# A column-sum kernel on one core: the first load takes nine rows instead of one and then eight, and the split of the last rows moves from 352 to 384 columns

## The chip, the cores and the metric

The kernel runs on one core of a Trainium2 chip. The metric is the device time in microseconds; the time before is 628.3 us (three runs, 628.29 to 628.32). A second number comes with every run: the span, from the first to the last instruction that the profiler records. It is printed to 0.1 us, and before's time is some 1.8 us longer than its span (628.3 against 626.5).

## The reference

```python
grad_output = np.random.randn(32, 1024, 2048).astype(np.float32)

def reference(grad_output):
    return np.sum(grad_output, axis=(0, 1)).astype(np.float32)
```

32,768 rows of 2048 fp32, 268.4 MB, are summed into one row. A row is 8 KB.

## The kernel before

SyncE issues all loads. A load of m rows per partition gives every partition m rows that follow each other in memory, so it is 128 pieces of m x 8 KB. A ring of three slots of eight rows takes 30 tiles; VectorE adds each tile into itself and carries two rows over to the next tile. One odd row (the "head") lies at the start of slot 2, where the first tile looks for the rows carried over. Fifteen rows per partition follow the tiles: VectorE adds seven of them, TensorE the other eight and VectorE's sum (products with a column of ones). The last three are loaded in a left part and a right part, so that little is left to do after the last byte.

```python
LEFT = ((0, 424, 0), (424, 424, 1), (848, 424, 2), (1272, 424, 3))
RIGHT = ((1696, 176, 2), (1872, 176, 3))
...
    ring = const_pool.tile([P, SLOTS * TILE * D], fp32)
...
    def load(m, dst, lane, after=None, first=None, lo=0, hi=D):
        ...
        src = flat[first : first + P * m].rearrange("(p m) d -> p m d", p=P)[:, :, lo:hi]
        loads.append((dst.rearrange("p (m d) -> p m d", m=m), src, lane, after))

    head_at = 2 * TILE
    load(1, rows(head_at, 1), head_in)
    for k in range(TILES):
        s = k % SLOTS
        load(TILE, rows(s * TILE, TILE), slot_in[s], (vec, k - 1) if k >= 2 else None)
...
    nc.vector.memset(psum[:], 0.0).then_inc(zero, 1)
    nc.vector.memset(rows(head_at + 1, WIDE - 1), 0.0)
    nc.vector.wait_ge(head_in, 16)
    with nc.vector.Fori(0, LOOPS):
        for s in range(SLOTS):
            at, before = s * TILE, (s - 1) % SLOTS * TILE
            take(nc.vector, slot_in[s])
            settle()
            vadd(at, rows(before, WIDE), WIDE).then_inc(vec, 1)
            ...
```

## Time and profile before

| what | before |
|---|---|
| time, span | 628.3 us, 626.5 us |
| first DMA issued, first packet | 0.89 us, 1.92 us |
| tile 0 in, on the first and on the last of 16 DMA engines | 24.65 us, 25.16 us |
| last load in, on the first and on the last engine | 622.46 us, 622.93 us |

Rows 2 to 4 come from the trace's packet records (start, duration, size) and from its records of semaphore increments: a load's semaphore rises once for each of the 16 DMA engines, so the trace tells when each engine's share of a load was in. The next lines are the timeline of before after the last load; columns are start, duration, engine and line, operation, and in brackets the idle time in front with what ended it.

```profile
622.97 0.09 PEld L199 LDWEIGHTS psum<-ring,ones 128*1 128x1 f32 x4 [0.22 <-DMA ring<-in_grad_output_dram]
623.21 0.64 SPq L232 DMA_DIRECT2D out_dram<-ring  x1
623.47 0.33 DVE L230 COPY ring<-psum 1x176 f32<-1x176 f32 x1 [3.28 <-PE psum L199]
623.51 0.30 ACT L230 COPY ring<-psum 1x176 f32<-1x176 f32 x1 [0.33 <-PE psum L199]
623.90 0.37 SPq L233 DMA_DIRECT2D out_dram<-ring  x1
```

The weight load of TensorE (PEld) at 622.97 us waited for a DMA: it starts 0.04 us after the last engine's share of the last load.

### The profile page before, as it was taken

The page shows a single profiled execution, that of the slowest core. Times are in us where ns is not written, and L with a number is a line of the kernel's source. Part 1 is how long each engine was busy: PE and PEld are TensorE (multiplying, and loading weights), DVE is VectorE, ACT ScalarE, POOL GpSimd, SP SyncE. Part 2 cuts the span into 40 slices and gives each one's busy share as a digit, 9 for nine tenths or more (in the row PEclk, how much of TensorE's full clock was granted, in tenths as well). Part 3 has the DMA queues.
Part 4 walks back from the last instruction along what each step waited for, and adds up shares of the span by engine and source line. Part 5 has one row for each costly group of instructions (what it writes and reads, how often), then busy time and mean ns, then how long its engine had stood idle before and what let it go on. Part 6 is the DMA issues. An engine that isn't in the chain of part 4 may idle for free. (4 is left out here: it accounts for less than half of the span.)

```text
span 626.5 us, 563 instructions
## 1 busy us (share of the span) xinstructions
PE 11.3 (2%) x108; PEld 3.4 (1%) x108; DVE 547.7 (87%) x102; ACT 2.3 (0%) x4; POOL 0.3 (0%) x5
## 2 busy tenths in 40 slices
PE   0000000000000000000000000000000000000007
PEld 0000000000000000000000000000000000000002
DVE  1389888899888898888988889888899888899996
ACT  0000000000000000000000000000000000000000
POOL 0000000000000000000000000000000000000000
PEclk9999999999999999999999999999999999999999
DMA  9999999999999999999999999999999999999997
GB/s 402 402 469 402 469 402 469 402 469 402 464 406 460 410 423 448 418 452 414 456 402 469 402 469 402 469 402 469 402 469 402 464 406 439 431 423 448 427 410 303
DMA packets 5755, 268.46 MB, mean 429 GB/s; under 512 B 629, under 2 KB 1018, under 8 KB 1402
## 3 DMA queue, kind: packets, MB, share of 16 engines
q1 hardware_dynamic: 5754, 268.45, 99.2%
q8 instruction: 1, 0.02, 0.0%
HBM read 268.44 MB, written 0.01 MB: 429 GB/s over the span
## 5 line engine op out<-in xcount | busy, mean ns | idle before, releaser
L122 DVE TENSOR_TENSOR ring<-ring 128x4096 f32<-128x4096 f32 (+2 forms) x93 | 528.9, 5687 | 71.0 <-DVEq L116 63.7
L199 PE MATMUL psum<-ring,ones 128*1 128x424 f32 (+1 forms) x108 | 11.3, 513 | 612.1 <-DMA ring<-in_grad_output_dram 612.0
L180 DVE TENSOR_TENSOR ring<-ring 128x6784 f32<-128x6784 f32 (+5 forms) x6 | 15.8, 2646 | 0.2
L199 PEld LDWEIGHTS psum<-ring,ones 128*1 128x1 f32 x108 | 3.4, 89 | 619.7 <-DMA ring<-in_grad_output_dram 614.2
L230 DVE COPY ring<-psum 1x176 f32<-1x176 f32 x1 | 0.3, 334 | 3.3 <-PE psum L199 3.3
L225 ACT COPY ring<-psum 128x424 f32<-128x424 f32 x1 | 0.5, 512 | 620.3 <-PE psum L199 620.3
L142 DVE MEMSET ring<- 128x2048 f32 x1 | 1.8, 1765 | 0.4 <-issue 0.4
L141 DVE MEMSET psum<- 128x1024 f32 x1 | 0.9, 912 | 1.2 <-POOLq L125 1.2
L222 ACT ACT_TABLE_LOAD x1 | 1.3, 1283 | 0.9 <-PEq L252 0.9
L230 ACT COPY ring<-psum 1x176 f32<-1x176 f32 x1 | 0.3, 300 | 0.3 <-PE psum L199 0.3
L222 ACT COPY warm<-ones 1x1 f32<-1x1 f32 x1 | 0.2, 190 | 0.0
L252 POOL MEMSET const-bfloat16-1.0<- 128x1 bf16 x1 | 0.1, 101 | 0.0
L252 POOL MEMSET const-uint8-127<- 128x1 uint8 x1 | 0.1, 101 | 0.0
L129 POOL MEMSET ones<- 128x1 f32 x1 | 0.1, 99 | 0.5 <-POOLq L125 0.5
L252 POOL MEMSET const-float32-0.0<- 128x1 f32 x1 | 0.1, 98 | 0.2 <-issue 0.2
L252 POOL MEMSET const-float32-1.0<- 128x1 f32 x1 | 0.1, 98 | 0.0
## 6 DMA issues: line engine op xcount, KB each, us to landing
ring<-in_grad_output_dram SPq DMA_DIRECT2D x1, 7168.0 KB, 33.3
ring<-in_grad_output_dram SPq DMA_DIRECT2D x1, 3072.0 KB, 21.8
ring<-in_grad_output_dram SPq DMA_DIRECT2D x1, 2048.0 KB, 26.4
ring<-in_grad_output_dram SPq DMA_DIRECT2D x1, 1696.0 KB, 30.0
ring<-in_grad_output_dram SPq DMA_DIRECT2D x1, 1024.0 KB, 4.9
ring<-in_grad_output_dram SPq DMA_DIRECT2D x1, 848.0 KB, 31.3
ring<-in_grad_output_dram SPq DMA_DIRECT2D x3, 176.0 KB, 31.1
ring<-in_grad_output_dram SPq DMA_DIRECT2D x30, 34.1
```

The costliest lines, as they stand in the source:

```text
L122: return nc.vector.tensor_add(out=rows(at if to is None else to, n), in0=rows(at, n), in1=other)
L129: nc.gpsimd.memset(ones[:], 1.0).then_inc(one, 1)
L141: nc.vector.memset(psum[:], 0.0).then_inc(zero, 1)
L142: nc.vector.memset(rows(head_at + 1, WIDE - 1), 0.0)
L180: add = nc.vector.tensor_add(out=x, in0=x, in1=grid[:, m:n, lo:hi])
L199: mat = nc.tensor.matmul(sums[lo], lhsT=ones[:], rhs=ring[:, x : x + n], start=start, stop=then is not None)
L222: nc.scalar.copy(out=warm[:], in_=ones[0:1, :])._wait_ge(one, 1)
L225: nc.scalar.copy(out=res, in_=psum[:, :n])._wait_ge(mm_left, len(LEFT)).then_inc(left, 1)
L230: copy(out=dst, in_=sums[lo])._wait_ge(mm_right, i + 1).then_inc(right, 1)
L252: nc = _bacc.Bacc("TRN2", target_bir_lowering=False, num_devices=1)
```

## The change

The first load takes nine rows at once into a store with one row of room ahead of the ring, on tile 0's semaphore; VectorE copies the odd row to where the first tile looks for it. That saves a DMA and a semaphore. And the right part of the last three rows is 384 columns wide, which puts the starts and ends of both parts on multiples of 512 B (1664 x 4 B = 13 x 512 B).

```diff
-LEFT = ((0, 424, 0), (424, 424, 1), (848, 424, 2), (1272, 424, 3))
-RIGHT = ((1696, 176, 2), (1872, 176, 3))
+LEFT = ((0, 416, 0), (416, 416, 1), (832, 416, 2), (1248, 416, 3))
+RIGHT = ((1664, 192, 2), (1856, 192, 3))
...
-    ring = const_pool.tile([P, SLOTS * TILE * D], fp32)
+    store = const_pool.tile([P, (1 + SLOTS * TILE) * D], fp32)
+    head, ring = store[:, :D], store[:, D:]
...
-    head_in, more_in = tc.alloc_semaphore("head"), tc.alloc_semaphore("more")
+    more_in = tc.alloc_semaphore("more")
...
     head_at = 2 * TILE
-    load(1, rows(head_at, 1), head_in)
-    for k in range(TILES):
+    load(1 + TILE, store[:, : (1 + TILE) * D], slot_in[0])
+    for k in range(1, TILES):
...
-    nc.vector.wait_ge(head_in, 16)
+    nc.vector.wait_ge(slot_in[0], 16)
+    nc.vector.tensor_copy(out=rows(head_at, 1), in_=head)
```

Nine rows are 73,728 B per partition, and the built kernel moves them as two pieces of 36,864 B.

## The prediction

> **What bounds the kernel now.** I read four views, in this order: the page's strip of 40 slices with the DMA totals under it, the groups by line and form, who waited for whom, and the chain that ended last. The strip first, because it tells at once whether one resource is full from end to end:
>
> ```profile
> DVE  1389888899888898888988889888899888899996
> DMA  9999999999999999999999999999999999999997
> DMA packets 5755, 268.46 MB, mean 429 GB/s; under 512 B 629, under 2 KB 1018, under 8 KB 1402
> HBM read 268.44 MB, written 0.01 MB: 429 GB/s over the span
> ```
>
> The reader is to see that the DMA row has no slice under 9 but the last, and that the whole input, 268.44 MB, is read once. VectorE is nearly as full, so the second view must show which of the two sets the pace:
>
> ```profile
> L122 DVE TENSOR_TENSOR ring<-ring 128x8192 f32<-128x8192 f32 x30 | 260.8, 8692 | 2.6
> L122 DVE TENSOR_TENSOR ring<-ring 128x4096 f32<-128x4096 f32 x58 | 256.7, 4425 | 67.3 <-DVEq L116 63.7 <-DMA ring<-in_grad_output_dram 1.5
> ```
>
> A tile of eight rows costs VectorE three adds: 4.43 + 8.69 + 4.43 = 17.5 us, 17.71 us with the drains between them. The timeline and the waits give the spacing of the tiles:
>
> ```profile
> 25.34 17.71 DVE L122 TENSOR_TENSOR ring<-ring 128x4096 f32<-128x4096 f32 x3 [21.01 <-DVEq L116]
> 44.69 17.71 DVE L122 TENSOR_TENSOR ring<-ring 128x4096 f32<-128x4096 f32 x3 [1.64 <-DVEq L116]
> 64.05 17.71 DVE L122 TENSOR_TENSOR ring<-ring 128x4096 f32<-128x4096 f32 x3 [1.65 <-DVEq L116]
> ...
> DVE ring L122 <- DVEq L116: 63.7, 27, 21.0
> ```
>
> Tiles start 19.36 us apart, and a tile's bytes are 128 x 65,536 = 8.389 MB, so the stream runs at 8.389 / 19.36 = 433 GB/s. VectorE needs 17.71 of the 19.36 us and stands still for 1.65 us at the wait for the slot (the sequencer's wait on L116 is the wait for a load's semaphore, so "DVEq" here means DMA). The stages at the two ends could still hold a hole in the stream; the busy time by stage says no:
>
> ```profile
> 6.00:44.69 38.69, 0.00 (x0) 0.00 (x0) 17.54 (x3) 0.00 (x0) 0.00 (x0) 1.00 1.00 434
> 44.69:547.66 502.97, 0.00 (x0) 0.00 (x0) 456.12 (x79) 0.00 (x0) 0.00 (x0) 1.00 1.00 434
> 547.66:590.00 42.34, 0.00 (x0) 0.00 (x0) 41.08 (x10) 0.00 (x0) 0.00 (x0) 1.00 1.01 435
> ```
>
> The last two columns are the DMA share and the GB/s: 434, 434 and 435. So the span is a start, then 268.44 MB at about 434 GB/s = 618.5 us, then a tail. The chain shows the tail:
>
> ```profile
> 590.30 31.29 DMA ring<-in_grad_output_dram
> 621.59 0.04 issue
> 621.64 1.85 PE psum L199 x20
> 623.49 0.02 issue
> 623.51 0.30 ACT ring L230
> ```
>
> PE is not the limit in it. The timeline has PE still idle 0.22 us for a load before the last two products at 622.97. In the trace's semaphore records the last row of the right piece is in at 622.93. From there to the end of the span are 3.6 us: product, copy, output DMA, closing barrier. The start: the first DMA is issued at 0.89 us, its first packet is recorded at 1.92 us. The run's 628.3 us stands 1.8 us over the 626.5 us span, which I leave as it is.
>
> [...] The trace shows little to win: the packet records give 0.258 us for 6784 B and 0.060 us for 1408 B, while a line through the 65,536 B packet (2.421 us) and the 8192 B packet (0.309 us) predicts 0.257 and 0.059 us. [...]
>
> **The change part by part.**
>
> Part A, the first load. Removed: one DMA of 128 packets of 8 KB, and its semaphore. The nine rows come as 128 x 2 pieces of 36,864 B. Bytes per DMA engine in these nine rows: before 8 x 8192 + 8 x 65,536 = 589,824 B in 16 packets; after 16 x 36,864 = 589,824 B in 16 packets. Time per engine from the packet line (7.3 ns + 0.03683 ns per byte): before 8 x 0.309 + 8 x 2.421 = 21.84 us, after 16 x 1.365 = 21.84 us. The difference is nil, less one semaphore write of 9 ns. The ramp can differ: before, the engines finished their 8 packets 3.0 to 3.5 us after 1.92 us, against 8 x 0.309 = 2.47 us of pure transfer, so the ramp cost 0.5 to 1.0 us, of which the first read's delay (first packets 1.2 us instead of 0.31) is most. It is paid once either way. A DMA of two pieces per partition also takes SP longer to issue (0.67 us for the two-row load of the tail, 0.43 us for one-piece loads), so the first packet may start 0 to 0.25 us later. I put part A at +0.1 us, from -0.3 to +0.4.
>
> Part B, the copy. [...] The first add moves from 25.34 to about 26.8 us. What hangs on it: the load of tile 2, which waits for that add and is issued at 29.8 us; that becomes 31.2. But the tile 1 load in front of it fills the DMA until 44.5 us, 13 us later, so the stream doesn't see it. On VectorE the 1.64 us of idle before tile 1 shrinks to about 0.2 us [...]. On the path: 0.
>
> Part C, the cut. Bytes of the six last loads are the same. Left packets: 24 per engine, each 128 B smaller, so the left rows land 24 x 128 x 0.0368 = 0.11 us earlier; the right ones bring the same back, and the last landing stays. VectorE's final adds: 32 columns x 7 move from the left chain to the right one (0.23 us), the end of the two together stays at 620.19 us, far ahead of 622.93. After the last landing: two products of 192 instead of 176 columns, 2 passes x 16 columns x 0.83 ns (starts of passes lie 0.149 us apart at 176 and 0.355 at 424) = +0.03 us; the two copies of 16 more elements +0.02 us. Against it, the left output is issued about 0.13 us earlier, so SP, which came free only 0.05 us before the right output's issue at 623.90 us, is no longer the later of the two. Net 0.0 us, from -0.1 to +0.1.
>
> Sum: +0.1 + 0 + 0.0 = +0.1 us on 628.3, less the semaphore [...]. I take 628.3.
>
> **The rivals.** R1: the merged load is a real saving, because a small first load cost a bubble. For it: the head landed 4.9 us after issue for 2.4 us of bytes. Against it: the packets of tile 0 begin at 4.97 us, before the last of the head has landed at 5.8, so the stream had no hole. It would give 627.6 to 627.9. R2: VectorE becomes the bound, since its work starts later and it has only 8% of slack. For it: 17.71 of 19.36 us. Against it: the delay is paid once, 26 more waits of 1.65 us follow, and the late issue has 13 us in hand. It would give at most +1.5 us, if nothing recovered. R3: two pieces per partition, or rows 73,728 B apart instead of 65,536, make the first 9.4 MB slower, say by a twentieth of 22 us: 629.4. Nothing in the profile speaks for it; the two-row load of the tail ran at its packets' rate. R4: the aligned cut makes the last 3 MB faster and the tail shorter: at best 0.1 us.
>
> **Range and chances.** The terms that don't cancel are the ramp (-0.3 to +0.4) and the tail (-0.1 to +0.1); runs of before differ by 0.03 us. Range 627.8 to 628.8. Two per cent is 12.6 us, more than start and tail together, and no rival comes near it: faster 0.01, within 0.98, slower 0.01.
>
> **What would show it.** Right: first add near 26.8 us, a copy of 1.2 us [...] just ahead of it; idle before tile 1 near 0.2 us, before tile 2 up to the usual 1.65 us; tile spacing 19.36 us; the DMA share 1.00 in the same stages; the last wait of PE still for a load, near 622.97 us. Wrong: tiles lastingly further apart than 19.36 us, the first add after 28 us (R3), a wait of SP for VectorE with the DMA share under 1 near 44 us (R2), or the first landing well before 25 us (R1).

With them go the argument that the stream could run no faster than its 434 to 435 GB/s (that this is a limit is not shown), the reasons for expecting something of an aligned cut, and the terms of part B for the length of the copy and the entry of the loop: together some 1.46 us, by which the first add was to move from 25.34 to 26.8 us. The sum came to +0.1 us for part A and nothing for B and C. From the 628.4 us that this makes, one semaphore write was taken off (9 ns, the median of the 4 B packets in before) and one term more. That gave the 628.3.

## More of the kernel before

The difference between the first and the last engine I call the spread.

## The result

The changed kernel takes 629.03 us (median of 6 runs, 628.87 to 629.71), before in the same rounds 628.29 us (628.14 to 628.32). The ratio is 1.0014, with a 95% interval of 1.0001 to 1.0027. Ratios here are the mean time of one kernel's runs over that of the other's of the same rounds, so not quite the ratio of the medians quoted. Within 2% was right. The time was not: 629.03 lies above the range of 627.8 to 628.8, 0.7 us over the 628.3 foreseen.

The page of after, strip and totals:

```profile
DMA  9999999999999999999999999999999999999996
HBM read 268.44 MB, written 0.01 MB: 428 GB/s over the span
```

The same stream, 268.44 MB, as full as before, but 428 instead of 429 GB/s over the span. The busy time by stage of after says whether the middle runs slower:

```profile
44.69:547.66 502.97, 0.00 (x0) 0.00 (x0) 456.30 (x79) 0.00 (x0) 0.00 (x0) 1.00 1.00 434
```

It doesn't: 434 GB/s at a share of 1.00, as before. So the loss was made at the ends. The timeline of after, start:

```profile
25.85 1.23 DVE L147 COPY store<-store 128x2048 f32<-128x2048 f32 x1 [21.52 <-DMA store<-in_grad_output_dram]
27.16 17.71 DVE L125 TENSOR_TENSOR store<-store 128x4096 f32<-128x4096 f32 x3
45.36 17.71 DVE L125 TENSOR_TENSOR store<-store 128x4096 f32<-128x4096 f32 x3 [0.49 <-DVEq L119]
64.72 17.71 DVE L125 TENSOR_TENSOR store<-store 128x4096 f32<-128x4096 f32 x3 [1.65 <-DVEq L119]
```

Before, VectorE took tile 0 at 25.34 us; here its first work on it, the copy, begins at 25.85, already half a microsecond late. Tile 1 starts at 45.36 instead of 44.69, tile 2 at 64.72 instead of 64.05: 0.67 us late each. The spacing is 19.36 us as ever, so the delay neither grows nor shrinks. And it is not VectorE's doing, which again waits 0.49 us for tile 1 and 1.65 us for tile 2. The chain of after that ended last:

```profile
592.56 31.30 DMA store<-in_grad_output_dram
623.86 0.04 issue
623.90 0.54 PE psum L203 x4
624.44 0.02 issue
624.47 0.31 ACT store L234
```

And the last weight load, from the timeline of after:

```profile
623.90 0.09 PEld L203 LDWEIGHTS psum<-store,ones 128*1 128x1 f32 x4 [0.47 <-DMA store<-in_grad_output_dram]
```

It came at 622.97 us before. The last DMA ends at 623.86 us, 0.93 us after that of before (622.93). The span of the profiled run is 627.3 us, 0.8 over before.

The records of the semaphores show where the 0.67 us come from, and how 0.93 us became of them. All times in us:

```
                              first engine   last engine   spread
tile 0 in, before                24.65          25.16       0.52
tile 0 in, after                 24.69          25.83       1.14
tile at about 586 in, before    585.85         586.33       0.49
tile at about 586 in, after     585.90         587.00       1.11
last load in, before            622.46         622.93       0.47
last load in, after             622.73         623.86       1.13
```

The fastest engine is as early as before. The slowest is 0.67 us later after the first load, and still is 560 us later: the trace has 16 landings for every tile, the gaps between them were not evened out (1.14 us at tile 0, 1.11 at about 586 us), and the last weight load waits for the slowest (landed 623.86, weight load 623.90). The records don't name the engines, but the 16 times of one load, put in order, keep their distances from tile 0 to the tile at about 586 us to within 0.05 us, in before as in after. The packet records show the beginning of this. In after the engines start their first packet between 2.00 and 3.23 us and end it between 3.91 and 5.05 us, and from there each needs 1.364 us per packet, without exception but one. A packet of 36,864 B takes 1.36 us in the stream; the first ones took up to 2.70 us. The ends of the first packets lie 1.13 us apart, which is the spread at tile 0.

The other 0.26 us come after the tile at 586 us. From there to the last load but one the slowest engine takes 36.25 us (36.20 before), and from that to the last load 0.61 us (0.40 before). Most of the latter is not in the packets: the last one of after ends 0.60 us before its semaphore rises, the last one of before 0.43 us. Why the last rise comes later I don't know; the section on the prediction compares the other profiles.

### The profile page after: what moved, and what is told of

It reads as the page before. It is cut to its first block, busy times and chain, and to the rows that moved or that the text cites. A ratio compares the mean times of both kernels' runs of the same rounds, so it can differ in the third digit from the quotient of the medians.

```text
span 627.3 us, 563 instructions
## 1 busy us (share of the span) xinstructions
PE 11.8 (2%) x108; PEld 3.3 (1%) x108; DVE 549.0 (88%) x103; ACT 2.3 (0%) x4; POOL 0.3 (0%) x5
## 3 DMA queue, kind: packets, MB, share of 16 engines
HBM read 268.44 MB, written 0.01 MB: 428 GB/s over the span
## 5 line engine op out<-in xcount | busy, mean ns | idle before, releaser
L125 DVE TENSOR_TENSOR store<-store 128x4096 f32<-128x4096 f32 (+2 forms) x93 | 528.9, 5687 | 48.9 <-DVEq L119 41.5
L203 PE MATMUL psum<-store,ones 128*1 128x416 f32 (+1 forms) x108 | 11.8, 523 | 612.6 <-DMA store<-in_grad_output_dram 612.6
L184 DVE TENSOR_TENSOR store<-store 128x6656 f32<-128x6656 f32 (+5 forms) x6 | 15.8, 2646 | 0.2
L203 PEld LDWEIGHTS psum<-store,ones 128*1 128x1 f32 x108 | 3.3, 90 | 620.7 <-DMA store<-in_grad_output_dram 615.1
L145 DVE MEMSET store<- 128x2048 f32 x1 | 1.8, 1765 | 0.4 <-issue 0.4
```

Source lines behind the costliest of these rows:

```text
L125: return nc.vector.tensor_add(out=rows(at if to is None else to, n), in0=rows(at, n), in1=other)
L184: add = nc.vector.tensor_add(out=x, in0=x, in1=grid[:, m:n, lo:hi])
L203: mat = nc.tensor.matmul(sums[lo], lhsT=ones[:], rhs=ring[:, x : x + n], start=start, stop=then is not None)
```

## The experiments

The first theory ("ramp"): the loss arises while the engines take up their first packets. Rivals: the tail ("cut"), and VectorE's later start ("copy"). Eighteen kernels ran in five calls (on chips 13, 5, 5, 12 and 10), each in five rounds beside before. The mean span and the time less the span are over the five runs, for before over nine; the last three columns are of the one profiled run, which is the first of each list. In all four kernels with the merged load in 36 KB pieces (after, e1, e7, e13) that run has the longest span of its list (once shared), so their profiles show more than the mean loss. The diffs are cut: where a load gets a source of its own, the `src` argument of `load` and the row counter are left out. "Nine rows in" is the landing of the last of the first nine rows on the last engine.

| run | median time us | mean span us | over before of the same call | time less span (median) | nine rows in us | spread us | last load in us |
|---|---|---|---|---|---|---|---|
| before, first profile | 628.30 | | | 1.74 | 25.16 | 0.52 | 622.93 |
| after, 6 runs | 629.03 | 627.08 | | 1.96 | 25.83 | 1.14 | 623.86 |
| before, call 1 | 628.31 | 626.40 | | 1.89 | | | |
| e1 merged load only | 628.60 | 626.76 | +0.36 | 1.90 | 25.60 | 0.84 | 623.52 |
| e2 copy only | 628.59 | 626.42 | +0.02 | 2.11 | 25.09 | 0.51 | 622.89 |
| e3 cut only | 628.34 | 626.52 | +0.12 | 1.80 | 25.13 | 0.28 | 623.12 |
| e4 pitched head | 628.18 | 626.42 | +0.02 | 1.78 | 25.10 | 0.61 | 622.85 |
| before, call 2 | 628.31 | 626.42 | | 1.90 | | | |
| e5 tile first | 628.45 | 626.64 | +0.22 | 1.80 | 25.17 | 0.42 | 622.96 |
| e6 nine small | 628.93 | 626.94 | +0.52 | 1.93 | 25.51 | 0.37 | 623.35 |
| e7 after again | 628.84 | 626.96 | +0.54 | 1.92 | 25.69 | 0.92 | 623.77 |
| e8 null | 628.26 | 626.44 | +0.02 | 1.79 | 25.16 | 0.48 | 622.93 |
| before, call 3 | 628.29 | 626.46 | | 1.81 | | | |
| e9 halves | 628.76 | 626.64 | +0.18 | 2.16 | 25.17 | 0.34 | 623.04 |
| e10 two of 32 KB | 628.35 | 626.58 | +0.12 | 1.81 | 25.45 | 0.67 | 623.20 |
| e11 pitched tile | 628.59 | 626.72 | +0.26 | 1.86 | 25.41 | 0.75 | 623.21 |
| e12 right 512 | 628.58 | 626.72 | +0.26 | 1.86 | 25.08 | 0.35 | 623.07 |
| before, call 4 | 628.31 | 626.54 | | 1.80 | | | |
| e13 merged again | 628.65 | 626.72 | +0.18 | 1.95 | 25.54 | 0.89 | 623.53 |
| e14 halves again | 628.54 | 626.50 | -0.04 | 2.09 | 25.19 | 0.48 | 622.94 |
| e15 two waits | 628.37 | 626.46 | -0.08 | 1.92 | 25.11 | 0.62 | 622.88 |
| e16 head in 4 KB | 629.10 | 627.30 | +0.76 | 1.80 | 25.96 | 1.01 | 623.73 |
| before, call 5 | 628.34 | 626.44 | | 1.84 | | | |
| e17 after, halves | 628.74 | 626.68 | +0.24 | 2.11 | 25.26 | 0.54 | 623.19 |
| e18 after, 1 + 8 | 628.68 | 626.62 | +0.18 | 2.05 | 25.35 | 0.79 | 623.40 |

The intervals, about 0.0013 to either side, hold most differences of this table. So I lean on means of spans, on repeats, and on pairs that differ in one thing. Spans of one kernel differ by 0.1 to 0.3 us from run to run for before (0.5 in call 4), by 0.3 to 0.5 us where the merged load is in.

### Call 1: the parts alone

**e1**, the merged load and the copy with the old cut:

```diff
 (after)
-LEFT = ((0, 416, 0), ...   RIGHT = ((1664, 192, 2), ...
+LEFT = ((0, 424, 0), ...   RIGHT = ((1696, 176, 2), ...
```

> The nine-row first load and the copy of the odd row, with the old cut (352). Ramp theory (the loss arises while the 16 DMA engines take up their first packets, and each engine keeps its delay to the end): the slowest engine's share of the first nine rows lands 0.4 to 0.7 us later than before (25.6 to 25.9 us against 25.16), the delay is the same at the last landing, time +0.4 to +0.7 us over before, 628.7 to 629.0. Cut theory (the loss is in the tail): +0.1 or less, 628.2 to 628.4.

Measured: span +0.36 us, time 628.60. Its timeline:

```profile
25.62 1.23 DVE L147 COPY store<-store 128x2048 f32<-128x2048 f32 x1 [21.29 <-DMA store<-in_grad_output_dram]
26.93 17.71 DVE L125 TENSOR_TENSOR store<-store 128x4096 f32<-128x4096 f32 x3
...
623.56 0.09 PEld L203 LDWEIGHTS psum<-store,ones 128*1 128x1 f32 x4 [0.37 <-DMA store<-in_grad_output_dram]
```

Tile 0 is 0.44 us late (25.60 against 25.16), the end of the stream 0.59 us (623.56 against 622.97). The ramp is seen with the cut undone. The median time, 0.3 us up, is a little under the range that the theory gave, and the delay grew by 0.15 us to the end, which it did not foresee.

**e2**, the copy alone: the head has its own DMA again, but lands ahead of the ring and is copied.

```diff
 (before)
+    store = const_pool.tile([P, (1 + SLOTS * TILE) * D], fp32)
+    head, ring = store[:, :D], store[:, D:]
-    load(1, rows(head_at, 1), head_in)
+    load(1, head, head_in)
...
     nc.vector.wait_ge(head_in, 16)
+    nc.vector.wait_ge(slot_in[0], 16)
+    nc.vector.tensor_copy(out=rows(head_at, 1), in_=head)
```

> Before, with the odd row loaded ahead of the ring by its own DMA and copied into it by VectorE once tile 0 is in. Copy theory (the later start of VectorE costs time): +0.3 us or more. Ramp and cut theories: a copy of 1.2 us, the first add at 26.5 us instead of 25.3, idle before tile 1 about 0.4 us, and the time as before within 0.1 us.

```profile
25.18 1.23 DVE L146 COPY store<-store 128x2048 f32<-128x2048 f32 x1 [20.85 <-DMA store<-in_grad_output_dram]
26.49 17.71 DVE L123 TENSOR_TENSOR store<-store 128x4096 f32<-128x4096 f32 x3
44.62 17.71 DVE L123 TENSOR_TENSOR store<-store 128x4096 f32<-128x4096 f32 x3 [0.42 <-DVEq L117]
```

Inside the span all came as expected: the first add 1.15 us later, tile 1 on time, span +0.02 us. The copy theory falls. But the time is 628.59, 0.28 us up, all of it outside the span (2.11 us at the median instead of 1.89). No theory had that; see e15.

**e3**, the cut alone:

```diff
 (before)
-LEFT = ((0, 424, 0), ...   RIGHT = ((1696, 176, 2), ...
+LEFT = ((0, 416, 0), ...   RIGHT = ((1664, 192, 2), ...
```

> Before with the right piece at 384 columns, nothing else. Cut theory: +0.5 us or more. Ramp theory: the packets of 6656 B save only some 2 ns each and those of 1536 B cost 5 to 7 ns more than the 1408 B ones (that is what the profile of after has), so over 24 of each per engine +0.1 us; time +0.05 to +0.2 us.

```profile
623.16 0.09 PEld L199 LDWEIGHTS psum<-ring,ones 128*1 128x1 f32 x4 [0.39 <-DMA ring<-in_grad_output_dram]
```

The stream ends at 623.16 here, 0.19 us after that of before, although tile 0 was 0.03 us early: from the ninth row's landing to the last load's it took 597.99 us, against 597.77 before. The span is 0.12 us up, the time 0.03 us. A cost of the expected order, and far from the 0.7 us of the cut theory. The packet records say why it isn't nil: 6656 B take 257 ns on the mean where the 6784 B took 258.4, and 1536 B take 67.6 where 1408 B took 60.1. With 24 packets of each per engine that is -0.03 and +0.18 us. So the cut on multiples of 512 B showed no gain beyond size: 128 B are worth 4.7 ns by the slope of the prediction's packet line (an estimate from before's packets of 8 and 64 KB), and the left packets got 1.4 ns faster, the right ones 7.5 ns slower.

**e4**, two loads as before, but cut out of the same nine-row blocks that after reads, so that the 8 KB packets lie 72 KB apart:

```diff
 (before)
-    load(1, rows(head_at, 1), head_in)
-    for k in range(TILES):
+    nine = flat[: P * (1 + TILE)].rearrange("(p m) d -> p m d", p=P)
+    load(1, rows(head_at, 1), head_in, first=0, src=nine[:, :1, :])
+    load(TILE, rows(0, TILE), slot_in[0], first=0, src=nine[:, 1:, :])
+    for k in range(1, TILES):
```

> Two loads as before (one row in 8 KB packets, then eight rows in 64 KB packets), but both out of the nine-row blocks that after reads: the 8 KB packets start 72 KB apart and span 9.4 MB instead of 1 MB. Size theory (a first packet of 36 KB is what widens the spread of the engines): as before, spread 0.5 us, 628.2 to 628.4. Address theory (the first reads lie too far apart): spread about 1.1 us and +0.4 to +0.7 us.

```profile
25.27 17.71 DVE L126 TENSOR_TENSOR ring<-ring 128x4096 f32<-128x4096 f32 x3 [20.94 <-DVEq L120]
```

Tile 0 is taken at 25.27 us, as in before (25.34), span +0.02 us, time 628.18. That the first reads of 8 KB lie 72 KB apart cost nothing that these spans show.

### Call 2: size of the first packets, or number of pieces

**e5**: the two loads of before in the other order, `load(TILE, rows(0, TILE), slot_in[0])` ahead of `load(1, rows(head_at, 1), head_in)`, so that the engines start on 64 KB.

> Before with the first two loads in the other order: tile 0 (one piece of 64 KB per partition) first, then the odd row in 8 KB packets. Size theory (each engine's delay grows with the size of the packet it starts on): spread of the first landing at least that of the merged load alone (0.84 us), the last landing 0.4 to 0.8 us after that of before, the span +0.4 to +0.8 us. Pieces theory (two pieces per partition in one DMA delay some engines): as before, spread 0.5 us, span 626.3 to 626.5 us.

A miss for both theories: the spread stays at 0.42 us and the profiled landing at 25.17, but over five runs the span is 0.22 us up.

**e6**: the merged load, with rows dealt to partitions so that each gets nine separate packets of 8 KB.

```diff
 (e1)
-    load(1 + TILE, store[:, : (1 + TILE) * D], slot_in[0])
+    nine = flat[: P * (1 + TILE)].rearrange("(m p) d -> p m d", p=P)
+    load(1 + TILE, store[:, : (1 + TILE) * D], slot_in[0], src=nine)
```

> The merged nine-row load with the old cut, but rows given to partitions so that each partition gets nine packets of 8 KB instead of two of 36 KB. Size theory: spread back to 0.5 us; against that 72 packets per engine instead of 16, 7.3 ns each, +0.4 us for every engine alike; span +0.3 to +0.5 us with a first landing that is later for the fastest engine too. Pieces theory: spread 0.8 us or more, so span +0.7 us or more.

Span +0.52 us with a spread of only 0.37 us. By an estimate from the prediction's packet line, 0.41 us of it are the 56 further packets per engine (56 x 7.3 ns); 0.1 us is left. So nine pieces of 8 KB per partition in one DMA did not widen the spread (0.37 us, before 0.52). The pieces theory in its plain form falls.

**e7**, the changed kernel unedited, and **e8**, before with a comment:

> The changed kernel once more, on the chip of these runs. If its parts add up (merged load +0.36 us of span, cut +0.12) the mean span is 0.4 to 0.55 us over before; if the loss of the six runs on record (+0.68 us of span) is right and the parts work on each other, 0.6 to 0.75.

> Before with one comment added: the noise from program to program. The time must be as before within 0.1 us; were it 0.2 us or more off, the +0.28 us of the kernel with the copy alone, whose span did not change, would be no finding.

The changed kernel repeats, with a span of +0.54 us, at the upper end of what its parts give when added, and 628.84 us. The null kernel stands at before, 628.26 us and 626.44 us, so a new program as such cost nothing here.

### Call 3: the same packets in one DMA or two

**e9**: the very packets of e1, 36 KB each from the same addresses, but the first pieces of all partitions in one DMA and the second pieces in another.

```diff
 (e1)
-    load(1 + TILE, store[:, : (1 + TILE) * D], slot_in[0])
+    nine = flat[: P * (1 + TILE)].rearrange("(p m) d -> p (m d)", p=P)
+    half = (1 + TILE) * D // 2
+    for i, lane in enumerate((head_in, slot_in[0])):
+        load(1, store[:, i * half : (i + 1) * half], lane, first=0, src=nine[:, i * half : (i + 1) * half])
...
+    nc.vector.wait_ge(head_in, 16)
     nc.vector.wait_ge(slot_in[0], 16)
```

> The merged load alone, but issued as two DMAs, one per 36 KB piece: the same bytes, packets and addresses, one piece per partition in each DMA. If the widened spread belongs to two pieces per partition in one DMA: spread about 0.5 us and a mean span at most 0.15 us over before. If it belongs to the packets of 36 KB or their addresses: as the merged load alone, spread 0.8 to 0.95 us, mean span +0.3 to +0.5 us.

```profile
25.26 1.23 DVE L154 COPY store<-store 128x2048 f32<-128x2048 f32 x1 [20.93 <-DMA store<-in_grad_output_dram]
```

The copy starts at 25.26 us instead of 25.62: the nine rows are in at 25.17, as in before, spread 0.34. The span is +0.18 us, half of e1's and between the two expectations.

**e10**, e5 with tile 0 in two pieces of 32 KB from rows 4 MB apart, and **e11**, e5 with tile 0 and the odd row out of the nine-row blocks, so in 64 KB packets 72 KB apart:

```diff
 (e5)
-    load(TILE, rows(0, TILE), slot_in[0])
 e10
+    tile0 = flat[: P * TILE].rearrange("(h p m) d -> p h (m d)", h=2, p=P)
+    load(TILE, rows(0, TILE).rearrange("p (h n) -> p h n", h=2), slot_in[0], first=0, src=tile0)
 e11
+    nine = flat[: P * (1 + TILE)].rearrange("(p m) d -> p (m d)", p=P)
+    load(TILE, rows(0, TILE), slot_in[0], first=0, src=nine[:, D:])
```

> Tile 0 first, as in the run with the tile ahead of the odd row, but in two pieces of 32 KB per partition from rows 4 MB apart, in one DMA. Two pieces theory: spread 0.8 us or more, mean span +0.3 us or more. Otherwise about 0.4 us and +0.2 us, as with one piece of 64 KB.

> Tile 0 first in packets of 64 KB, but 72 KB apart, out of the nine-row blocks that after reads (then the odd rows of these blocks). If the pitch of 72 KB together with large packets makes the spread: 0.8 us or more, mean span +0.3 us or more. If not, 0.4 us and +0.2 us, as with the pitch of 64 KB.

Neither expectation was met. Neither run is as bad as the merged load nor quite as good as before: spread 0.67 and 0.75 us, span +0.12 and +0.26 us. e11 and e4 move the same bytes in the same packets from the same addresses; only the order of the two DMAs differs, and e4, with the small packets first, has +0.02. The same holds for e5 and before. So in both pairs a start on 64 KB goes with 0.2 us more.

**e12**, the cut moved further, right part 512 columns:

> Before with the cut moved further, right piece 512 columns: packets of 6144 and 2048 B. From the packet line (7.3 ns + 0.0368 ns per byte) the stream ends when it did. If any departure from 352 columns costs by size: +0.3 us of span, since the right rows' two products and copies after the last landing grow by 80 columns (0.13 + 0.15 us). If packets of 1536 B are slow in themselves (67 ns where the line says 64), packets of 2048 B are again at the line, 83 ns, and the last landing is at 622.9 us.

```profile
623.11 0.09 PEld L199 LDWEIGHTS psum<-ring,ones 128*1 128x1 f32 x4 [0.53 <-DMA ring<-in_grad_output_dram]
623.74 0.42 DVE L230 COPY ring<-psum 1x256 f32<-1x256 f32 x1 [3.61 <-PE psum L199]
```

Packets of 2048 B take 86 to 87 ns where the line said 83, and 6144 B 238 to 239 where it said 234. So 1536 B is not special. My line, good to 1 ns at the old sizes of 6784 and 1408 B, is 2 to 5 ns too low at 6656, 6144, 2048 and 1536 B. The stream ends at 623.11 and the products and copies behind it grow: from there to the copy are 0.63 us, against 0.50 in before, and VectorE's copy takes 0.42 us instead of 0.33. Span +0.26 us.

### Call 4: repeats, the time outside the span, and smaller packets

**e13** and **e14** are e1 and e9 again.

> The merged load alone once more. If its cost is the start of the stream and varies from run to run: mean span +0.25 to +0.5 us over before, single spans between 626.5 and 627.0 us, spread in the profile 0.6 to 1.2 us, the last landing later by what tile 0's landing is later. If the +0.36 us was chance: below +0.15 us.

> The two DMAs of 36 KB pieces once more. If two pieces per partition in one DMA matter beside the size of the first packets: mean span +0.1 to +0.25 us again, clearly under the merged load's. If not: the same mean span as the merged load, +0.25 to +0.5 us. Time less span 2.1 us again.

Both missed their ranges: e13 has +0.18 us, between chance and the +0.25 foreseen, and e14 -0.04. Before's own spans ran up to 626.9 us in this call, so the difference to before is of less use. Merged against halves: 626.72 against 626.50 us. Over both calls the ten spans of each have means of 626.74 and 626.57 us: 0.17 us for issuing the same packets as one DMA. The profiles agree, 25.54 to 25.60 us against 25.17 to 25.19. In the four profiles of a merged load (e1, e7, e13 and after) two or three engines took 2.4 to 2.8 us for their first packet; in the three of halves (e9, e14, e17) none took over 2.35 us. Two DMAs differ in more than the pieces in each: there are two issues, and the first packet starts at 1.91 to 1.93 us instead of 1.98 to 1.99.

**e15**: before with two waits added on VectorE, both long fulfilled.

```diff
 (before)
+    nc.vector.wait_ge(one, 1)
+    nc.vector.wait_ge(zero, 1)
     nc.vector.wait_ge(head_in, 16)
```

> Before with two waits added on VectorE that are long fulfilled, no copy, no other load. If two more instructions cost time outside the span: span 626.4 us as before, time less span 2.1 us instead of 1.85, time about 628.55 us. If it was the copy or the other allocation: 628.3 us as before.

A partial miss: the built program has one more instruction, 564 instead of 563, and not two, and the time outside the span is 1.92 us, 0.1 more than before's, not 2.1. But this puts all kernels in order. By VectorE's instructions over before, the medians of time less span are: none (e3, e4, e5, e8, e10, e11, e12, e16, and before in all calls) 1.78 to 1.90 us; one (after, e1, e6, e7, e13, e15) 1.90 to 1.96; two (e2, e9, e14, e17, e18) 2.05 to 2.16. e16 has one more on SyncE instead and stays at 1.80. Against before of the same call, two more give 0.21 to 0.35 us, one more 0.01 to 0.15: the step is clear for two, and for one not beyond the 0.1 us to which spans are printed. What happens outside the span in that time no profile shows. So for after the one instruction more may stand for some 0.1 us of its loss; that is argued from this order, not shown.

**e16**: the head of before in two DMAs of 4 KB packets.

```diff
 (before)
-    load(1, rows(head_at, 1), head_in)
+    for i in range(2):
+        lo, hi = i * D // 2, (i + 1) * D // 2
+        load(1, ring[:, head_at * D + lo : head_at * D + hi], head_in, first=0, src=flat[:P, lo:hi])
...
-    nc.vector.wait_ge(head_in, 16)
+    nc.vector.wait_ge(head_in, 32)
```

> Before with the first row loaded in two DMAs of 4 KB packets. If the delay at the start goes on falling with the size of the first packets: mean span 0.05 to 0.15 us under before (eight more packets per engine cost 0.06 us of it back). If 8 KB is small enough: as before, or 0.06 us more.

```profile
26.13 17.71 DVE L127 TENSOR_TENSOR ring<-ring 128x4096 f32<-128x4096 f32 x3 [21.80 <-DVEq L121]
```

A clear miss: the first half of the head is in at 4.81 us, but the second only at 6.42, 0.6 us after the head of before (5.81). So most of the loss is there when the head ends; tile 0 is 0.8 us late, the spread 1.01 us, the span +0.76 us. The packets of 4 KB took 0.16 us at the median and up to 0.64 us. So smaller was not better here. The eight packets of 8 KB happen to suit this start; why 4 KB don't, I did not find.

### Call 5: the changed kernel itself

**e17** is the changed kernel with the nine rows in two DMAs of the same 36 KB pieces (the edit of e9), **e18** with one row in 8 KB and eight rows in 64 KB packets out of the same blocks, copy and cut unchanged.

```diff
 (after) e18
-    load(1 + TILE, store[:, : (1 + TILE) * D], slot_in[0])
+    nine = flat[: P * (1 + TILE)].rearrange("(p m) d -> p (m d)", p=P)
+    load(1, head, head_in, first=0, src=nine[:, :D])
+    load(TILE, rows(0, TILE), slot_in[0], first=0, src=nine[:, D:])
```

> The changed kernel with its first load issued as two DMAs of the same 36 KB pieces. If one DMA with two pieces per partition is what delays some engines: first copy near 25.3 us instead of 25.6 to 25.9, mean span 626.55 to 626.75 us (the cut's 0.12 and at most 0.1 of start) against 627.0 of the changed kernel; time less span about 2.1 us, as both have two more instructions on VectorE. If not: mean span 626.9 or more.

> The changed kernel with its nine-row blocks loaded as one row in 8 KB packets, then eight rows in 64 KB packets. Mean span 626.5 to 626.65 us: before and the 0.12 us of the cut, nothing of the start; time about 628.65 us with 2.1 us outside the span.

The copy in e17:

```profile
25.35 1.23 DVE L154 COPY store<-store 128x2048 f32<-128x2048 f32 x1 [21.02 <-DMA store<-in_grad_output_dram]
```

Mean spans of 626.68 and 626.62 us, as expected, against 627.03 of the changed kernel (its 11 spans, of other calls): 0.35 to 0.4 us come back though the copy and the cut stay. What is left over before (626.44 in this call), 0.18 to 0.24 us, is the cut's 0.12 and some 0.1 us more. The times, 628.74 and 628.68, gain less: 2.11 and 2.05 us lie outside the span, and both have two more instructions on VectorE than before. None of the kernels beats before beyond the noise: the lowest, e4, has 628.18 us at before's span.

## Why the prediction was right or wrong

- **What bounds the kernel** was right. From the nine rows to the tile at about 586 us the slowest engine takes 561.13 to 561.28 us in all twenty profiles, and the loads set the end.
- **Part B** was right: a copy of 1.228 us, where the prediction had 1.2, the first add delayed, tile 2's load issued later, and no effect on the stream. Alone it gives +0.02 us of span (e2). The first add came at 27.16 us instead of 26.8, because the load itself was late (25.83 us against 25.16); it starts 0.08 us after the copy's end, so the entry of the loop was put too high.
- **Part A failed**, at this step: "The difference is nil ... The ramp can differ ... It is paid once either way", put at +0.1 us with -0.3 to +0.4. Bytes and packet times per engine were right (1.364 us against 1.365), and the fastest engine did land as before. The longer issue was right too: the first packet starts at 1.98 to 1.99 us instead of 1.92. The ramp was treated as one number for the core. It is 16 numbers, and the end follows the largest: nine rows in at 25.54 to 25.83 us on the last engine in four profiles, against 25.08 to 25.16 in the six that start as before does (before, e2, e3, e8, e12, e15), so 0.4 to 0.7 us late. The profile of before had shown the quantity (0.5 us between engines, unchanged from 25 to 622 us) and I had it on the table only as 3.0 to 3.5 us for the head. (Its "first packets 1.2 us" is also a misreading: only four engines took that long for theirs.) In the mean of spans the merged load costs 0.36 and 0.18 us in two calls with the old cut. With the cut of after, undoing it gives back 0.35 to 0.4 us.
- **Part C** was mis-sized: net 0.0 us foreseen, 0.12 us measured in span (e3), 0.2 us in the length of the stream in its profile. The term "the right ones bring the same back" took single packets from a line that is 2 to 5 ns too low at the new sizes; over 48 packets that is 0.1 to 0.2 us. The other terms behind it came out near what was put: in e3 the copies take 0.35 and 0.31 us instead of 0.33 and 0.30, from the last landing to the first of them are 0.56 us instead of 0.54, and SP is free at 623.81 us, 0.26 before the right output's issue; but the left output is issued only 0.04 us earlier, not 0.13.
- **"I leave as it is"**, said of the 1.8 us outside the span, was a term of zero for what went up to 1.96 us at the median. That may be 0.1 us, and is not well known.
- **The sum**: merged load 0.2 to 0.4, cut 0.12, outside some 0.1, so 0.4 to 0.6 us against 0.53 (e7) and 0.74 us in the medians. The latter is not covered. One run of each, the profiled one of e1 and e13 and the last of the six of after, took 0.5 to 0.7 us more outside the span than its fellows. Only kernels with the merged load had such runs, and I don't know why.
- **The rivals**: R1 (a saving) and R2 (VectorE becomes the bound) were rightly refused. R3 named the right place, two pieces per partition and rows 72 KB apart, with a wrong mechanism (slower bytes); "nothing in the profile speaks for it" was too quick. R4 (a gain from the aligned cut) had the wrong sign: e3 has +0.12 us of span.
- **The range** was too narrow because its ramp term came from one profile of another first load.

What stays open: what happens in the first packets that makes two or three engines take 2.4 to 2.8 us for theirs, most others 1.8 to 2.3, when both pieces come in one DMA. Size of packets (e5, e6, e11), distance (e4) and number of pieces (e6, e10) each alone fail to give it; the same packets in two DMAs (e9, e14, e17) take half of it or more away. Open too is the stream's surplus of 0.15 to 0.2 us between the nine rows and the last load in e1 and e13 (597.92 and 597.99 us, against 597.77 in before with the same cut). The records show where it lies: not on the way, but in the last load alone. From its last packet's end to its last semaphore rise it is 0.58 to 0.60 us in the four profiles of the merged load in 36 KB pieces, and 0.42 to 0.52 in the sixteen others, e16 with nearly the spread of after among them (0.43). Only profiled runs can show it. The surplus of e3 is of another kind: 0.12 of its 0.22 us came between the tile at 586 us and the last load, as longer packets would have it.

## What to carry to other kernels

In this stream, with a DMA share of 1.00 from 44.69 to 547.66 us, a delay that some DMA engines had at the start was still there at the end: the spread was 0.52 us at tile 0 and 0.47 at the last load in before, 1.14 and 1.13 in after (it varied most in e1, with 0.84, 0.67 at 586 us and 0.84, and in e18, with 0.79 and 0.57). So look at the spread between the engines in the semaphore records, not only at the mean rate. Merging two loads into one saved nothing here, where the stream had no hole (0.36 and 0.18 us of span more in e1 and e13), and it widened that spread (0.84 and 0.89 us); try the order of sizes at the start, and measure with repeats, since the effect scatters by more than it amounts to in one run. A sum of near-cancelling terms over many small packets is only as good as its single packet times multiplied by their number.
